# Six column tiles in the first pass, x over three queues, and a residual added on TensorE: one hybrid decoder step

## The chip, the core and the metric

The kernel runs on one core of a Trainium2 chip. The metric is the device time of one execution in microseconds (us). The engines are TensorE (PE, with PEld for its weight loads), VectorE (DVE), ScalarE (ACT), GpSimd (POOL) and SyncE (SP). SP, ACT and POOL can issue DMAs, each from a queue of its own.

## What is computed

One step of a one-layer decoder on 280 tokens: 16 meta tokens, 256 prompt tokens and 8 single tokens of running sequences. Everything is float32.

```python
u = rmsnorm(h, pre_mix_g)
proj = u @ w_in                      # 2048 -> 6672: z, x/B/C, dt, q, k, v, g
xbc = silu(causal_conv(xbc))         # width 4
# 16 Mamba-2 SSD heads beside 4 retention heads, chunked; states are returned
h = h + rmsnorm(mix @ w_out, post_mix_g)
f = rmsnorm(h, pre_ffn_g)
f = (silu(f @ w_gate) * (f @ w_up)) @ w_down     # 2048 -> 5632 -> 2048
h = h + rmsnorm(f, post_ffn_g)
```

## The kernel before

**Layout and products.** Features lie on the 128 partitions and tokens along the free dimension. Each float32 product is made of three fast matmuls (`three`, L129 to L133): weight and input are split into a rounded part (`hi`) and the rest (`lo`), and hi·hi, hi·lo and lo·hi are added up in PSUM. The weights are one stream of chunks of 8 blocks of 128x128 (`Stream.block`, L112). SP loads a chunk into `raw` (four buffers), ACT casts it to `hi` (L122), and DVE subtracts to get `lo` (L123); `hi` and `lo` have three buffers each. The first chunk is cut into four pieces.

**First pass.** `gemm("xb", ...)` (L336) makes 13 column tiles: `dt`, four tiles of B and C, eight of x. For its first columns it runs with `outer=4`: k is the outer loop, and for each of the 16 slabs of the input four columns are advanced at once in four PSUM banks, so that PE can start when the first slab is there. The other nine columns run one by one, 48 matmuls each. `prep(k)` (L163) loads two slabs of x on SP (L169), scales and splits each (ACT L170, DVE L171), squares them on ACT, and adds the squares up on POOL (L178). After the last slab two float32 matmuls (`pr`, L208) give the token norms, and `rbc` scales every eviction. `do_dt` (L247) is a generator: its long DVE chain on `dt`, transposes, a small DMA to memory and back (`lcd`, then four broadcasts `lcb`, L293 to L296), and `wj` (L304) are put in at columns 7, 8 and 9. `do_xbc` (L309) does the convolution of the other columns.

**Order of the work.** Each engine runs its instructions in one fixed order. A planner lays that order down ahead of time by priorities: program order, with some places moved ahead (`high_priority`, by 1500 for x and weights, 3000 for evictions). A wait on any engine holds back all that stands behind it there.

**Tail.** `gemm("d", ...)` (L883) makes 16 output columns; each eviction squares on ACT and scales on DVE into `o2` (L762, L763). `rstds` (L633, matmul L638) adds the squares up over the partitions and takes the root with Ln and Exp on ACT (L646, L648). Then the eight pairs of columns are multiplied by `rstd` (L895), the residual `hrs` is added (L903), and each pair is stored (L904, SP and ACT in turn). POOL does one of the eight multiplications and four of the eight additions, DVE the rest. The residual is loaded back from memory in eight loads (L888, issued by `load`, L85).

Of the kernel before, what the change touches and what calls it, by code (L numbers as in the profile page):

```python
# [15 lines left out]
P = 128  # L16
# [29 lines left out]
NEXTRA = 4  # L46
DECAY_ACT = False
WARM = 9
OUTF = 6


@with_exitstack
def hybrid_step(ctx: ExitStack, tc: tile.TileContext, wall, xT, pp, cc, dmask, cs, convst, ssm, ret,
# [16 lines left out]
    def slot(name, w=NA, n=4, dt=F32):  # L70
        return sp.tile([P, n, w], dt, name=name, tag="s")
# [12 lines left out]
    def load(out, in_):  # L84
        G.dma_start(out, in_)  # L85

    pps = cp.tile([P, NPP], F32, name="pps")
    nc.scalar.dma_start(pps, pp)
    ccs = cp.tile([P, NCC], F32, name="ccs")
    css = slot("css", NA, 2)  # L90

# [17 lines left out]
    class Stream:  # L109
        pos = 0  # L110

        def block(self):  # L112
            c, o = divmod(self.pos, CB)
            if o == 0:
                with tc.high_priority(offset=1500):
                    raw = st.tile([P, CB * P], F32, name=f"raw{c}", tag="raw", bufs=4)
                    self.hi = st.tile([P, CB * P], F32R, name=f"hi{c}", tag="hi")
                    self.lo = st.tile([P, CB * P], F32R, name=f"lo{c}", tag="lo")
                    w = CB * P // (4 if c == 0 else 1)
                    for f in range(0, CB * P, w):  # L120
                        nc.sync.dma_start(raw[:, f:f + w], wall[c, :, f:f + w])
                        A.copy(self.hi[:, f:f + w], raw[:, f:f + w])  # L122
                        V.tensor_tensor(self.lo[:, f:f + w], raw[:, f:f + w], self.hi[:, f:f + w].bitcast(F32), SUB)  # L123
            self.pos += 1
            return self.hi[:, o * P:(o + 1) * P], self.lo[:, o * P:(o + 1) * P]

# [33 lines left out]
    ul = [slot(f"ul{i}", dt=F32R) for i in range(4)]  # L160
    xsum = slot("xsum", NA, 2)

    def prep(k):  # L163
        i, j = divmod(k, 4)
        with tc.high_priority(offset=1500):
            for q in (j, j + 1):
                if k == 0 or q == j:
                    n = 1 if k == 0 else 2
                    nc.sync.dma_start(xs[i][:, q:q + n, :], xT[:, 4 * i + q:4 * i + q + n, :])  # L169
                A.activation(uh[i][:, q, :], xs[i][:, q, :], AF.Copy, scale=par("g_pre", 4 * i + q))  # L170
                V.scalar_tensor_tensor(ul[i][:, q, :], xs[i][:, q, :], par("g_pre", 4 * i + q),  # L171
                                       uh[i][:, q, :].bitcast(F32), MULT, SUB)
            if k == 0:
                A.activation(xsum, xs[i][:, j:j + 2, :], AF.Square)
            else:
                sq = slot(f"xq{k}", NA, 2)
                A.activation(sq, xs[i][:, j:j + 2, :], AF.Square)
                G.tensor_tensor(xsum, xsum, sq, ADD)  # L178

    ready = set()  # L180

# [23 lines left out]
    def token_norms():  # L205
# [12 lines left out]
    def pinned(out, in_):  # L218
        tc.keep_in_program_order(G.dma_start(out, in_))

    def const_loads():
        pace = cp.tile([P, 1], F32, name="pace0")
# [110 lines left out]
            do_xbc(m - 1, ps)  # L333

    held = {}
    gemm("xb", uin0, KT, NA, 0, 4, ev_first, outer=4, before=const_loads)  # L336
    for m in range(4, 13):
        gemm("xb", uin, KT, NA, m, m + 1, ev_first, pool=pm if m < 6 else pg)
        if 7 <= m < 10:
            next(held["dt"])  # L340
    load(oconv, cout.rearrange("p a b c -> p a (b c)"))
# [543 lines left out]
    hrs = []  # L885
    for k in range(0, KT, 2):
        hr = slot(f"hr{k}", NO, 2)
        load(hr, hd[:, k:k + 2, :])  # L888
        hrs.append(hr)
    pool_mul, pool_add = (7,), (0, 2, 4, 7)  # L890

    def scaled(n):
        ok = o2[n // 2][:, 2 * (n % 2):2 * (n % 2) + 2, :]
        e = G if n in pool_mul else V
        e.tensor_tensor(ok, ok, rstd.unsqueeze(1).to_broadcast([P, 2, NO]), MULT)  # L895

    scaled(7)
    for n in range(8):
        ok = o2[n // 2][:, 2 * (n % 2):2 * (n % 2) + 2, :]
        if n < 7:  # L900
            scaled(n)
        e = G if n in pool_add else V
        e.tensor_tensor(ok, ok, hrs[n], ADD)  # L903
        (nc.sync if n % 2 == 0 else nc.scalar).dma_start(yT[:, 2 * n:2 * n + 2, :], ok)  # L904


def _constants():
# [38 lines left out]
def _blocks(m, kouter=0):  # L946
    k, n = m.shape
    a = m.reshape(k // P, P, n // P, P).transpose(2, 0, 1, 3)
    if not kouter:
        return a.reshape(-1, P, P)  # L950
    return a.transpose(1, 0, 2, 3).reshape(-1, P, P)


def _layout(i):
    import numpy as np
    w = i["w_in"][0]
    z, xx, bb, cm = w[:, :1024], w[:, 1024:2048], w[:, 2048:2304], w[:, 2304:2560]
    dt, q, k, v, g = w[:, 2560:2576], w[:, 2576:3600], w[:, 3600:4624], w[:, 4624:5648], w[:, 5648:6672]
    first = np.concatenate([np.tile(dt, (1, 8)), bb, cm[:, :128]], 1)
    wo, wd = i["w_out"][0], i["w_down"][0]  # L960
    gu = np.stack([i["w_gate"][0].reshape(DM, FT, P), i["w_up"][0].reshape(DM, FT, P)], 2).reshape(DM, 2 * DFF)
    seq = [_blocks(first, 1), _blocks(np.concatenate([cm[:, 128:], xx], 1)), _blocks(k), _blocks(q), _blocks(v),
           _blocks(z), _blocks(g), _blocks(wo[:, :512], 1), _blocks(wo[:, 512:]), _blocks(gu[:, :P * OUTF], 1),
           _blocks(gu[:, P * OUTF:]), _blocks(wd)]
# [51 lines left out]
```

## Time and profile before

| | |
|---|---|
| median of three runs | 1280.14 us (1277.64 to 1282.41) |
| profiled execution | 1281.71 us, of which the span of the core 1279.9 us |
| PE, share of the span | 98% |
| DVE, ACT, POOL | 64%, 47%, 12% |
| chain that ended last | PE 95%, DMA 2%, DVE 1%, issue 1% |
| mean granted TensorE clock | 0.994 |

Busy shares are means over stages with different limits: where a stage waits is read from the waits and the timeline of that stage. Matmuls are pipelined, so that the rows show them overlapping; the pace is the distance between two starts.

### The profile page before, as it was taken

To read this page: it belongs to the slowest core of one execution; us is meant where nothing else is said; L and a number is where in the kernel's file an instruction comes from. 1 tells how busy PE (TensorE), PEld (TensorE's weight loads), DVE (VectorE), ACT (ScalarE), POOL (GpSimd) and SP (SyncE) were. 2 spreads that over 40 slices of the span, in tenths; PEclk is the share of its full clock that TensorE was granted. 3 is DMA by queue.
4 is the path that set the end of the run, shared out by engine and by line. 5 is a ranking of instruction groups with operands and counts; after the bars stand their busy time and mean duration, and the time that the engine had idled before them with its cause. 6 is when DMAs were issued, how large, how long until landed. Compare 5 with 4: busy or idle time off the path is not lost.

```text
span 1279.9 us, 24519 instructions
## 1 busy us (share of the span) xinstructions
PE 1254.4 (98%) x10078; PEld 1240.9 (97%) x10078; DVE 821.3 (64%) x1247; ACT 607.8 (47%) x826; POOL 153.1 (12%) x218
## 2 busy tenths in 40 slices
PE   8989999999999999999999999999999999999994
PEld 7989999999999999999999999999999999999994
DVE  7978779984775458566666666666666544444445
ACT  6665434445854446544444444444444433333331
POOL 3320001100001221101110110101101000000013
PEclk9999999999999999999999999999999999999997
DMA  8656347774466556577677766767676555555562
GB/s 271 206 190 215 121 147 260 273 260 144 136 214 230 182 180 217 183 244 245 229 236 247 246 231 231 248 215 248 214 247 229 183 181 181 182 182 181 181 223 93
DMA packets 74768, 266.41 MB, mean 208 GB/s; under 512 B 8528, under 2 KB 9440, under 8 KB 74656
## 3 DMA queue, kind: packets, MB, share of 16 engines
q1 hardware_dynamic: 60192, 214.17, 51.7%
q0 software_dynamic: 13744, 49.52, 10.7%
q8 instruction: 79, 1.29, 0.4%
q10 hardware_dynamic: 720, 1.16, 0.2%
q14 instruction: 33, 0.27, 0.1%
HBM read 246.15 MB, written 18.66 MB: 207 GB/s over the span
## 4 chain that ended last, share of the span: by engine, by line
PE 95%; DMA 2%; DVE 1%; issue 1%; SPq 0%; ACT 0%; POOL 0%; DVEq 0%; ACTq 0%
PE f L131 13%; PE f L133 13%; PE f L132 13%; PE d L132 7%; PE d L131 7%; PE d L133 7%; PE o L131 2%; PE o L132 2%; PE o L133 2%; PE xb L132 1%; PE xb L133 1%; PE xb L131 1%; PE k L131 1%; PE v L131 1%; PE v L132 1%; PE k L132 1%
## 5 line engine op out<-in xcount | busy, mean ns | idle before, releaser
L123 DVE TENSOR_TENSOR lo<-raw,hi 128x1024 fp32r<-128x1024 f32 (+1 forms) x405 | 492.3, 1217 | 357.8 <-ACT hi L122 353.1
L122 ACT CAST hi<-raw 128x1024 fp32r<-128x1024 f32 (+1 forms) x405 | 422.1, 1043 | 601.9 <-PE f L132 191.7
L131 PE MATMUL f<-fh,hi 128*128 128x264 f32 x1408 | 400.6, 285 | 0.0
L133 PE MATMUL f<-fh,lo 128*128 128x264 f32 x1408 | 399.3, 284 | 0.0
L132 PE MATMUL f<-fl,hi 128*128 128x264 f32 x1408 | 398.6, 283 | 0.0
L132 PEld LDWEIGHTS f<-fl,hi 128*128 128x128 f32 x1408 | 264.8, 188 | 0.3 <-issue 0.2
L131 PEld LDWEIGHTS f<-fh,hi 128*128 128x128 f32 x1408 | 264.8, 188 | 0.3 <-DVE f L863 0.2
L133 PEld LDWEIGHTS f<-fh,lo 128*128 128x128 f32 x1408 | 264.6, 188 | 0.0
L132 PE MATMUL d<-al,hi 128*128 128x264 f32 x704 | 200.2, 284 | 0.0
L131 PE MATMUL d<-ah,hi 128*128 128x264 f32 x704 | 199.7, 284 | 0.0
L133 PE MATMUL d<-ah,lo 128*128 128x264 f32 x704 | 199.4, 283 | 0.0
L131 PEld LDWEIGHTS d<-ah,hi 128*128 128x128 f32 x704 | 132.5, 188 | 0.0
L132 PEld LDWEIGHTS d<-al,hi 128*128 128x128 f32 x704 | 132.4, 188 | 0.0
L133 PEld LDWEIGHTS d<-ah,lo 128*128 128x128 f32 x704 | 132.3, 188 | 0.0
L131 PE MATMUL o<-mh,hi 128*128 128x264 f32 x256 | 72.8, 284 | 0.0
L132 PE MATMUL o<-ml,hi 128*128 128x264 f32 x256 | 72.6, 284 | 0.0
L133 PE MATMUL o<-mh,lo 128*128 128x264 f32 x256 | 72.4, 283 | 0.0
L869 POOL COPY pace<-f 128x1 f32<-128x1 f32 x25 | 28.6, 1144 | 362.2 <-DVE f L863 362.2
L858 DVE TENSOR_TENSOR f<-f,rhc 128x264 f32<-128x264 f32 x88 | 37.6, 432 | 49.1 <-PE f L133 48.8
L131 PE MATMUL xb<-uh,hi 128*128 128x280 f32 x208 | 61.8, 299 | 3.1 <-ACT hi L122 3.1
L133 PE MATMUL xb<-uh,lo 128*128 128x280 f32 x208 | 61.1, 297 | 3.4 <-DVE lo L123 3.4
L132 PE MATMUL xb<-ul,hi 128*128 128x280 f32 x208 | 61.7, 297 | 1.2 <-DVE ul L171 1.2
(296 smaller groups left out, 1983.2 us busy)
## 6 DMA issues: line engine op xcount, KB each, us to landing
raw<-in_dram SPq DMA_DIRECT2D x401, 512.0 KB, 3.6
rs<-in_dram POOLq DMA_DIRECT2D x16, 512.0 KB, 5.3
su<-in_dram POOLq DMA_DIRECT2D x16, 512.0 KB, 4.9
out_dram<-su POOLq DMA_DIRECT2D x16, 512.0 KB, 3.9
hb<-in_dram POOLq DMA_DIRECT2D x8, 512.0 KB, 5.9
hu<-in_dram POOLq DMA_DIRECT2D x8, 512.0 KB, 5.1
out_dram<-hu POOLq DMA_DIRECT2D x8, 512.0 KB, 4.1
lcb<-lcd POOLq DMA_DIRECT2D x4, 544.0 KB, 9.1
```

The costliest lines, as they stand in the source:

```text
L122: A.copy(self.hi[:, f:f + w], raw[:, f:f + w])
L123: V.tensor_tensor(self.lo[:, f:f + w], raw[:, f:f + w], self.hi[:, f:f + w].bitcast(F32), SUB)
L131: T.matmul(ps, hi, xhi, start=first, stop=False)
L132: T.matmul(ps, hi, xlo, start=False, stop=False)
L133: T.matmul(ps, lo, xhi, start=False, stop=last)
L858: V.tensor_tensor(t, ps, rhc, MULT)
L869: tc.keep_in_program_order(G.tensor_copy(pace, t[:, 0:1]))
```

## The change

In the first pass six columns are advanced at once (`OUTX = 6`; four PSUM banks of one pool and two of the other) and seven follow one by one; the weights are laid out to match. The first chunk is cut into three pieces. Slab 0 of x is loaded by SP, slabs 1 to 3 by ACT, the other twelve by POOL in pairs, each pair held back by a one-element copy on POOL that waits for the split of an earlier slab (`x_late`). The load of the parameters `pps` gets a high priority. The squares are added up by DVE instead of POOL.

In the tail the residual is loaded in four loads ahead of the last GEMM. For the first four pairs (eight columns) PE copies the residual into PSUM with an identity matmul and adds the scaled result with a second one, and ACT copies the sum back. DVE does all eight multiplications and the last four additions, POOL none. All stores go out from SP.

```diff
+OUTX = 6
+NPE = 4
@@ Stream.block
-                    w = CB * P // (4 if c == 0 else 1)
-                    for f in range(0, CB * P, w):
+                    cuts = (0, 2 * P, 4 * P, CB * P) if c == 0 else (0, CB * P)
+                    for f0, f1 in zip(cuts, cuts[1:]):
...
+    def x_loads():
+        nc.sync.dma_start(*xpart(0, 0, 1))
+        nc.scalar.dma_start(*xpart(0, 1, 2))
+        nc.scalar.dma_start(*xpart(0, 2, 4))
+    def x_late(k, parts):
+        pace = cp.tile([P, 1], F32, name=f"pacex{k}")
+        i, j = divmod(k, 4)
+        tc.keep_in_program_order(G.tensor_copy(pace, ul[i][:, j, 0:1].bitcast(F32)))
+        for p in parts:
+            pinned(*xpart(*p))
+    late = {0: ((1, 0, 2),), 1: ((1, 2, 4),), 2: ((2, 0, 2),), 4: ((2, 2, 4),), 6: ((3, 0, 2),), 8: ((3, 2, 4),)}
@@ prep
+            if k == 0:
+                x_loads()
...
-                    nc.sync.dma_start(xs[i][:, q:q + n, :], xT[:, 4 * i + q:4 * i + q + n, :])
...
+                if 4 * i + q in late:
+                    x_late(4 * i + q, late[4 * i + q])
...
-                G.tensor_tensor(xsum, xsum, sq, ADD)
+                V.tensor_tensor(xsum, xsum, sq, ADD)
@@ first pass
-    gemm("xb", uin0, KT, NA, 0, 4, ev_first, outer=4, before=const_loads)
-    for m in range(4, 13):
-        gemm("xb", uin, KT, NA, m, m + 1, ev_first, pool=pm if m < 6 else pg)
+    gemm("xb", uin0, KT, NA, 0, OUTX, ev_first, outer=OUTX, before=const_loads)
+    for m in range(OUTX, 13):
+        gemm("xb", uin, KT, NA, m, m + 1, ev_first, pool=pm if m == OUTX else pg)
@@ tail
+    hrs = []
+    for i in range(4):
+        hr = slot(f"hr{i}", NO)
+        load(hr, hd[:, 4 * i:4 * i + 4, :])
+        hrs.append(hr)
     ev, sums = ev_norm(o2, "g_pffn")
     gemm("d", ain, FT, NO, 0, KT, ev)
...
-    pool_mul, pool_add = (7,), (0, 2, 4, 7)
...
+    def residual(k):
+        sums_[k] = bank(f"h{k}", NO) if k % 2 else pg.tile([P, 512], F32, name=f"h{k}", tag="g")[:, :NO]
+        T.matmul(sums_[k], ident, hrs[k // 4][:, k % 4, :], start=True, stop=False)
+    for k in range(4):
+        residual(k)
+    for n in range(NPE):
+        scaled(n)
+        for k in (2 * n, 2 * n + 1):
+            ok = o2[k // 4][:, k % 4, :]
+            T.matmul(sums_[k], ident, ok, start=False, stop=True)
+            A.copy(ok, sums_.pop(k))
+        store(n)
+        for k in (2 * n + 4, 2 * n + 5):
+            if k < 2 * NPE:
+                residual(k)
+    for n in range(NPE, 8):
+        scaled(n)
+        ok = pair(o2, n)
+        V.tensor_tensor(ok, ok, pair(hrs, n), ADD)
+        store(n)
```

## Rows read from the trace of the kernel before

**Rows 1.** The waits of PE over the span: total us, times, longest us.
```profile
PE xb L133 <- DVE lo L123: 3.4, 1, 3.4
PE xb L131 <- ACT hi L122: 3.1, 2, 2.1
PE xb L132 <- DVE ul L171: 1.2, 2, 0.8
```
**Rows 2.** Timeline of PE, first pass: start, us, engine, line, operation; bracket: idle before.
```profile
4.55 0.38 PE L131 MATMUL xb<-uh,hi 128*128 128x280 f32 x1
...
11.42 0.40 PE L131 MATMUL xb<-uh,hi 128*128 128x280 f32 x1 [2.15 <-ACT hi L122]
...
13.30 0.29 PE L131 MATMUL xb<-uh,hi 128*128 128x280 f32 x1
...
17.94 0.29 PE L131 MATMUL xb<-uh,hi 128*128 128x280 f32 x1
...
35.30 1.10 PE L208 MATMUL pr<-xsum,ones 128*128 128x280 f32 x4
```
**Rows 3.** Timeline of ACT, first pass.
```profile
1.19 1.28 ACT L82 ACT_TABLE_LOAD   x1 [1.19 <-PEq L996]
3.52 0.53 ACT L170 ACTIVATE uh<-x,pps 128x280 fp32r<-128x280 f32 x1 [1.05 <-DMA pps<-in_dram]
...
10.33 1.04 ACT L122 CAST hi<-raw 128x1024 fp32r<-128x1024 f32 x1 [0.26 <-DMA raw<-in_dram]
```
**Rows 4.** Windows: stretch, its length, busy us by engine, PEclk, DMA share, GB/s.
```profile
3.00:9.00 6.00, 5.08 (x35) 4.71 (x34) 2.45 (x6) 3.27 (x9) 0.00 (x0) 1.00 0.83 231
9.00:10.00 1.00, 0.27 (x3) 0.04 (x1) 0.88 (x2) 1.00 (x3) 0.00 (x0) 1.00 1.03 417
```
**Rows 5.** Timeline of DVE and POOL, first pass.
```profile
9.12 0.93 DVE L171 SCALAR_TENSOR_TENSOR ul<-x,pps,uh 128x280 fp32r<-128x280 f32 x2 [1.36 <-ACT uh L170]
...
13.85 2.09 DVE L171 SCALAR_TENSOR_TENSOR ul<-x,pps,uh 128x280 fp32r<-128x280 f32 x2
...
14.22 1.40 POOL L178 TENSOR_TENSOR xsum<-xsum,xq 128x560 f32<-128x560 f32 x1 [2.71 <-ACT xq L177]
```
**Rows 6.** Waits between 78 and 97 us, then windows around that stall.
```profile
DVE wj L304 <- DMA lcb<-lcd: 6.2, 2, 3.9
...
89.10:92.50 3.40, 0.04 (x1) 0.00 (x0) 1.34 (x3) 3.37 (x6) 0.00 (x0) 1.00 0.11 43
92.50:96.40 3.90, 3.89 (x18) 3.90 (x19) 3.83 (x8) 3.49 (x6) 0.56 (x3) 0.56 0.74 190
```
**Rows 7.** A window of the columns made one by one, and its weight subtractions on DVE.
```profile
36.00:97.00 61.00, 57.64 (x429) 56.32 (x428) 52.30 (x116) 39.21 (x64) 14.34 (x40) 0.97 0.60 200
...
L123 DVE TENSOR_TENSOR lo<-raw,hi 128x1024 fp32r<-128x1024 f32 x17 | 20.7, 1223 | 3.4 <-ACT hi L122 3.3
```
**Rows 8.** Timeline of DVE and POOL in the tail.
```profile
1264.40 4.14 DVE L895 TENSOR_TENSOR p<-p,n5r 128x528 f32<-128x528 f32 x3 [1.24 <-ACT n5r L648]
...
1266.35 5.08 POOL L903 TENSOR_TENSOR p<-p,hr 128x528 f32<-128x528 f32 x3
...
1275.48 1.32 DVE L903 TENSOR_TENSOR p<-p,hr 128x528 f32<-128x528 f32 x2
```
**Rows 9.** The stores, from issue to landing.
```profile
DMA to landing us min/median/max: 2.0/2.1/2.2
```
**Rows 10.** PE after the last column of the output projection, and in the tail; ACT beside it.
```profile
476.67 1.03 PE L626 MATMUL ps<-vtok,ktok 128*128 128x256 f32 x4
477.69 0.71 PE L638 MATMUL n<-g_postq,ones 128*128 128x264 f32 x2
...
1262.24 0.39 ACT L762 ACTIVATE g_pffnq<-d 128x264 f32<-128x264 f32 x1 [7.87 <-PE d L133]
1262.69 0.71 PE L638 MATMUL n<-g_pffnq,ones 128*128 128x264 f32 x2
```
**Rows 11.** The loads of the residual: us of issue, first and last start.
```profile
L85 POOL DMA_DIRECT2D hr<-hd x8: 539/540/578, 1215.4 to 1249.2; - x8
```
**Rows 12.** A window of the tail.
```profile
1267.00:1270.00 3.00, 0.00 (x0) 0.00 (x0) 3.00 (x2) 0.00 (x0) 3.00 (x3) 0.51 0.24 90
```

More of the change, by code (lines that the diff above doesn't have):

```diff
@@ L85, in load, with pinned @@
         G.dma_start(out, in_)
+    def pinned(out, in_):
+        tc.keep_in_program_order(G.dma_start(out, in_))
     pps = cp.tile([P, NPP], F32, name="pps")
-    nc.scalar.dma_start(pps, pp)
+    with tc.high_priority(offset=6000):
+        nc.scalar.dma_start(pps, pp)
     ccs = cp.tile([P, NCC], F32, name="ccs")
@@ L118, in block @@
                     self.lo = st.tile([P, CB * P], F32R, name=f"lo{c}", tag="lo")
-                    w = CB * P // (4 if c == 0 else 1)
-                    for f in range(0, CB * P, w):
-                        nc.sync.dma_start(raw[:, f:f + w], wall[c, :, f:f + w])
-                        A.copy(self.hi[:, f:f + w], raw[:, f:f + w])
-                        V.tensor_tensor(self.lo[:, f:f + w], raw[:, f:f + w], self.hi[:, f:f + w].bitcast(F32), SUB)
+                    cuts = (0, 2 * P, 4 * P, CB * P) if c == 0 else (0, CB * P)
+                    for f0, f1 in zip(cuts, cuts[1:]):
+                        nc.sync.dma_start(raw[:, f0:f1], wall[c, :, f0:f1])
+                        A.copy(self.hi[:, f0:f1], raw[:, f0:f1])
+                        V.tensor_tensor(self.lo[:, f0:f1], raw[:, f0:f1], self.hi[:, f0:f1].bitcast(F32), SUB)
             self.pos += 1
@@ L161, in hybrid_step, with xpart @@
     xsum = slot("xsum", NA, 2)
+    def xpart(i, q0, q1):
+        return xs[i][:, q0:q1, :], xT[:, 4 * i + q0:4 * i + q1, :]
+    def x_loads():
[9 more added lines that the diff above has]
+    late = {0: ((1, 0, 2),), 1: ((1, 2, 4),), 2: ((2, 0, 2),), 4: ((2, 2, 4),), 6: ((3, 0, 2),), 8: ((3, 2, 4),)}
     def prep(k):
@@ L165, in prep @@
         with tc.high_priority(offset=1500):
+            if k == 0:
+                x_loads()
             for q in (j, j + 1):
-                if k == 0 or q == j:
-                    n = 1 if k == 0 else 2
-                    nc.sync.dma_start(xs[i][:, q:q + n, :], xT[:, 4 * i + q:4 * i + q + n, :])
                 A.activation(uh[i][:, q, :], xs[i][:, q, :], AF.Copy, scale=par("g_pre", 4 * i + q))
@@ L216, in token_norms @@
             A.mul(tabs[:, 2 + i, :], tabs[:, i, :], 1.0 / 16.0)
-    def pinned(out, in_):
-        tc.keep_in_program_order(G.dma_start(out, in_))
     def const_loads():
@@ L884, in hybrid_step, with pair, store @@
     (rstd,) = rstds("n5", [[sums["a"], sums["b"]]], 1.0 / DM, load_table=False)
[L885 to L889, printed above, removed]
-    pool_mul, pool_add = (7,), (0, 2, 4, 7)
-    def scaled(n):
[L893 to L904, printed above, removed]
+    def pair(tiles, n):
+        return tiles[n // 2][:, 2 * (n % 2):2 * (n % 2) + 2, :]
+    def scaled(n):
+        ok = pair(o2, n)
+        V.tensor_tensor(ok, ok, rstd.unsqueeze(1).to_broadcast([P, 2, NO]), MULT)
+    def store(n):
+        nc.sync.dma_start(yT[:, 2 * n:2 * n + 2, :], pair(o2, n))
+    sums_ = {}
+    def residual(k):
[15 more added lines that the diff above has]
+        scaled(n)
+        ok = pair(o2, n)
+        V.tensor_tensor(ok, ok, pair(hrs, n), ADD)
+        store(n)
 def _constants():
@@ L958, in _layout @@
     dt, q, k, v, g = w[:, 2560:2576], w[:, 2576:3600], w[:, 3600:4624], w[:, 4624:5648], w[:, 5648:6672]
-    first = np.concatenate([np.tile(dt, (1, 8)), bb, cm[:, :128]], 1)
+    xbc = np.concatenate([np.tile(dt, (1, 8)), bb, cm, xx], 1)
     wo, wd = i["w_out"][0], i["w_down"][0]
     gu = np.stack([i["w_gate"][0].reshape(DM, FT, P), i["w_up"][0].reshape(DM, FT, P)], 2).reshape(DM, 2 * DFF)
-    seq = [_blocks(first, 1), _blocks(np.concatenate([cm[:, 128:], xx], 1)), _blocks(k), _blocks(q), _blocks(v),
+    seq = [_blocks(xbc[:, :P * OUTX], 1), _blocks(xbc[:, P * OUTX:]), _blocks(k), _blocks(q), _blocks(v),
            _blocks(z), _blocks(g), _blocks(wo[:, :512], 1), _blocks(wo[:, 512:]), _blocks(gu[:, :P * OUTF], 1),
```

## The prediction, made before the changed kernel was seen

> **What bounds the kernel now.** I first read the engines' shares: PE is busy for 98% of the span, so a change can give back only what PE loses. The waits of PE [rows 1] list all of that between its first matmul and its last but for fragments: one wait of 3.4 us on a `lo` and four that add up to 4.3 us, all in the first pass. Then I read the timeline at the two ends. At the start [rows 2]: the first product begins at 4.55 us and the four-column phase ends at 35.30 us, where `pr` starts. From 13.30 to 17.94 us PE runs undisturbed: 12 blocks of three matmuls in 4.64 us, 0.129 us a matmul. The phase has 4 x 16 x 3 = 192 of them, 24.8 us; it took 30.75, so 6.0 us are lost (the waits above and small delays that are no wait on the list). At the other end [rows 8]: from 1264.40 us on, PE has nothing to do, and DVE works alone on the path until 1276.8 us; the last store lands some 2 us later [rows 9]. Between these ends the GEMMs hide everything else.
>
> **The first pass: what the start loses.** Of the 6.0 us, chunk 1 of the weights costs most. The first 24 matmuls need only chunk 0; the 25th starts at 11.42 us, since the chunk's cast began at 10.33 us, just when its load had landed [rows 2, 3]. Ideal would be 4.55 + 24 x 0.129 = 7.65 us, so 3.8 us are lost up to there and 6.0 - 3.8 = 2.2 us after it. With six columns a slab takes 18 matmuls, but chunk 0 still holds just 24 matmuls' work, so the start still hangs on when chunk 1 lands. Ahead of it the same bytes are needed as before. What can move is how densely they are carried: from 3 to 9 us the DMA engines were busy at 0.83 and moved 231 GB/s [rows 4], so 6 x 0.17 = 1.0 us of their time was unused. With SP freed of slabs 1 to 3 it issues chunk 1 some three issues sooner. I take 0.8 us; the bounds are 1.0 us and, if POOL's first late pair (slabs 4 and 5, asked for once slab 0 is split) now runs ahead of chunk 1, a loss of 280 KB at 231 GB/s, 1.2 us.
>
> This is a place where a rule speaks against the change. The Trainium skill ("DMA: Bandwidth & Descriptors", section "Rules for kernel authors") says that spreading loads over SP, ACT and GpSimd gives no bandwidth, as all run on the same 16 engines, and saves issue time alone. By that rule the 0.8 us would be nothing and the sum 0.8 us smaller, a rival below; the second row of the windows, 417 GB/s from the same single queue in the tenth microsecond, sides with the rule, the 0.83 of the first speaks for some issue time to be saved.
>
> **The first pass: after chunk 1.** Of the 2.2 us, 1.2 are waits on `ul` [rows 1], and the small delays beside them I put down to the same queue of DVE. Two `ul` take 0.93 us together while POOL is idle and 2.09 us while POOL adds squares [rows 5]. The change ends that: POOL's seven additions go to DVE. DVE's own price for one is bounded by its 128x528 additions in the tail, spaced 0.62 us when POOL was done and 1.8 when it was not [rows 8]; I take 0.7. Per slab DVE then does 0.75 of a chunk (1.22 us each [rows 7], so 0.92), one `ul` (0.47) and half an addition (0.35): 1.74 us of PE's 18 x 0.129 = 2.32. DMA needs 384 + 140 KB per slab, 231 GB/s against the 417 it can do. So both keep up, and I count 1.9 of the 2.2 us as saved. Six columns themselves remove no matmul: 624 stay 624.
>
> The rest of this part I cost at nothing, with its cover. ACT issues two loads of x ahead of its 1.28 us table load: 1.19 + 0.84 + 1.28 = 3.3 us, covered by the wait for `pps` until 3.52 us [rows 3]; 0.2 us are to spare. The six one-element copies on POOL stand ahead of the later pairs of x and of `const_loads`; each waits for a slab at least four ahead of the pair it releases, and a slab lasts PE 2.32 us, so a pair has over 8 us. First pass: 0.8 + 1.9 = 2.7 us saved, from -0.3 (late pair in the way, half of the rest) to 1.0 + 2.2 = 3.2.
>
> **The middle: a stall that the change moves.** At 89.1 us PE loses 3.4 us and then runs until 96.4 us at a mean granted clock of 0.56, half speed for most of it: 18 matmuls in 3.9 us instead of 2.3, 1.6 us more [rows 6]. Its `lo` stood on DVE behind `wj`, which waited 6.2 us for the `lcb` broadcasts. With six columns `dt` is evicted two columns, 12 us of PE work, later, less what the start gains; the chain through `dt`, `lcd` and `lcb` moves with it, toward the first k columns. The planner places `wj` anew, by its own idea of when `lcb` lands. Nothing shortens the chain, so I take the stall as unchanged: 0, bounded by -5.0 us (it vanishes) and by the second rival.
>
> **The tail.** DVE's 528-wide operation costs 1.8 us beside POOL and 0.62 to 0.70 alone [rows 8]. After the change POOL is still, and DVE has 8 multiplications and 4 additions: 12 x 0.62 + 0.08 = 7.5 us, from 1264.40 to 1271.9 instead of 1276.8: 4.9 us. The other branch: the first pair is ready at 1265.1; PE then has 8 sums and 4 residuals to do in float32. Two such matmuls (four records) took about 1.0 us in the middle, one alone 0.71 with its latency [rows 10]; at 0.45 each, 12 take 5.4 us, to 1270.5, and ACT's last copy 0.39 after that [rows 10]: 1271.1 with the gaps between. DVE ends last, but by 0.8 us only.
>
> Two things eat into the 4.9 us. The planner can slip residual matmuls in front of the last norm matmul, which waits for ACT's square: after the output projection it did so with two `ps` matmuls, and the norm matmul started a microsecond after they did [rows 10] instead of the 0.45 us that ACT's square alone takes here; I take 0.45 us. And stores: before they went out over 9 us and each landed 2.1 us after issue [rows 9]; now four or five of 264 KB follow within 2 us on SP alone, in order, so that one that waits for ACT holds those behind it. At the 300 to 400 GB/s of the start that is 0.7 to 0.9 us each; I take 0.6 us of queueing. Tail: 4.9 - 0.45 - 0.6 = 3.85 us saved; from 4.9 to 0.3 (fourth rival). The residual's loads move from 1215 us and later [rows 11] to before the last GEMM, on a POOL queue that is idle there: nothing, covered by 250 us of PE work.
>
> **Sum.** 2.7 + 0 + 3.85 = 6.55 us. The profiled execution took 1281.71 us, so 1275.2 for it; it lies 1.57 us above the median of 1280.14, so I forecast 1273.6 us. A measurement of this kernel tells 0.5%, 6.4 us, from no change: the line is at 1273.7, and the forecast stands on it. Its own range is 1272.0 (first pass and tail both at their good ends, 3.2 and 4.9) to 1276.6 (first pass at its bad end).
>
> **Rivals.** First, the stall in the middle goes away, because `wj` lands behind enough finished `lo`: 5.0 us more, 1268.6. For it: it hung on one ordering. Against: the chain is as long as before.
>
> Second, the other side: DVE falls behind in the columns made one by one. From 36 to 97 us it did 52.3 us of work, 20.7 of them 17 `lo` [rows 7]. Now seven columns remain, 14 `lo` (17.1 us) and the same 31.6 of other work: 48.7 us against 7 x 48 x 0.129 + 2.5 (the float32 matmuls between) = 45.9 of PE. It was ahead before and is now 2.8 us behind, and the 6.2 us wait comes on top: if PE must wait for both, 9.0 in place of 3.4, and half clock for as long again, it costs 5.6 + 1.6, and 1280.8 us is slightly slower than before. It decides as soon as the planner lets convolution work ahead of `lo`. Against it: `lo` has priority, and the convolutions can slide into the k columns.
>
> Third, the queues bring nothing and the start stays bound to chunk 1 at 11.4 us: 0.8 us less, 1274.4; with POOL's pair in its way and half of the DVE gain lost as well, 1276.6.
>
> Fourth, PE's clock falls in the tail. Before, with PE idle from 1263.4 us, the granted clock was 0.51 between 1267 and 1270 [rows 12], its 1.2 GHz level. The 12 float32 matmuls would take 0.9 us each, 10.8 in all, and end at 1276.5 with ACT's copy: the tail saves 0.3, and the time is 1277.2. Against it: the matmuls themselves keep PE busy from 1265 us on.
>
> **Chances.** Forecast 0.45, split about evenly at the line; first rival 0.15; second 0.15, a third of it slower by over 0.5% should waits add up beyond the price; third 0.15; fourth 0.10. Faster by over 0.5%: 0.22 + 0.15 + a third of the third rival, 0.05: 0.42. Slower by over 0.5%: 0.05. Within: 0.53. The range reaches from the first rival to the fourth and most of the second: 1268 to 1280.
>
> **What would show it.** `pr` at 35.30 + 12.4 - 2.7 = 45.0 us, with the 25th matmul near 10.6 us; `ul` at 0.47 us each throughout; no PE wait on `ul`. In the tail 12 DVE operations of 0.62 us and the last addition 7.5 to 8 us after `rstd`; stores that land within 3 us of it. I would be wrong if chunk 1 landed later than 10.3 us, if PE's total wait between 45 and 110 us differed much from 3.4 us, or if the last store came from ACT's copies instead of DVE.

## The result, and the profile after

| | before | after |
|---|---|---|
| median of the runs beside each other | 1279.37 us (1277.64 to 1282.41, 4 runs) | 1271.57 us (1271.00 to 1272.85, 4 runs) |
| profiled execution | 1281.71 us, span 1279.9 | 1271.0 us, span 1269.2 |
| mean granted TensorE clock | 0.994 | 1.0 |

The ratio is 0.9938, with an interval of 0.9917 to 0.9959: the changed kernel is 0.6% faster. The forecast was 1273.6 us, with 1268 to 1280 around it; the time came out 2.0 us below it. It also lies 0.4 us below the forecast's own range of 1272.0 to 1276.6; only the wider range, with the rivals in it, holds it.

First the engines' shares of after:

```profile
PE 1261.2 (99%) x10110; PEld 1247.3 (98%) x10110; DVE 812.7 (64%) x1254; ACT 605.2 (48%) x829; POOL 138.3 (11%) x214
```

PE is still the bound. What it loses has become less, and the list of its waits shows where (total us, times, longest us):

```profile
PE xb L137 <- ACT hi L128: 1.7, 2, 0.9
PE warm L113 <- DVE ones L111: 1.1, 1, 1.1
PE n L660 <- DVE rqs L714: 0.2, 1, 0.2
```

Beside [rows 1], both the wait on `lo` (3.4 us) and the waits on `ul` (1.2 us) are gone, and the one on the first casts fell from 3.1 to 1.7 us. That wait is another one now: both parts of it (0.93 and 0.74 us) are for the second and third piece of chunk 0, while ACT took up chunk 1, at 9.48 us, without waiting for its load. (The `warm` wait lies before the first product, in both kernels.)

To see how much each stage gave, I follow PE's timeline at the seams. After:

```profile
4.92 0.84 PE L137 MATMUL xb<-uh,hi 128*128 128x280 f32 x2
...
45.08 1.10 PE L233 MATMUL pr<-xsum,ones 128*128 128x280 f32 x4
...
92.32 0.29 PE L137 MATMUL k<-uh,hi 128*128 128x280 f32 x1
...
468.45 0.61 PE L660 MATMUL n<-g_posts,ones 128*128 128x264 f32 x2
...
479.78 0.47 PE L137 MATMUL f<-fh,hi 128*128 128x264 f32 x1
...
1000.00 0.28 PE L137 MATMUL d<-ah,hi 128*128 128x264 f32 x1
...
1255.79 0.60 PE L660 MATMUL n<-g_pffns,ones 128*128 128x264 f32 x2
```

The six-column phase (the slab phase: slab by slab, all its columns at once) ends at 45.08 us. Before, the four-column phase ended at 35.30 us [rows 2]; two more columns are 96 matmuls of 0.129 us, so the same point is 47.7 us. The table reads the other seams of the two profiled executions in the same way; its column "gained in the stage" is what the stage itself gave.

| seam | before | after | gained in the stage | forecast |
|---|---|---|---|---|
| end of the slab phase, `pr` (six columns) | 47.7 us | 45.08 us | 2.6 | 2.7 |
| first `k` matmul | 100.08 | 92.32 | 5.2 | 0 |
| norm after the output projection | 476.23 | 468.45 | 0.0 | 0 |
| first `d` matmul, after the `f` GEMM | 1005.67 | 1000.00 | -2.1 | 0 |
| last norm, after the `d` GEMM | 1261.99 | 1255.79 | 0.5 | 0 |
| end of the span | 1279.93 | 1269.23 | 4.5 | 3.85 |

The first row is no fixed size. The old start ended its slab phase at 35.30, 34.94 and 34.69 us in three profiles (before, and two runs below that share its first pass), the new one at 44.87 to 46.10 us in five; on the scale of the table that is a gain of anything from 1.0 to 2.8 us.

The rows add up to 10.7 us, but the medians differ by 7.8 only. The two profiled executions are not typical in the same way: that of before, 1281.71 us, lies 1.6 us above the 1280.14 it was read against (2.3 above 1279.37), that of after 0.6 below its median: 10.7 - 2.3 - 0.6 = 7.8.

**The middle.** The windows of after (length, busy us by engine, PEclk, DMA share, GB/s) show no stall between 78 and 98 us:

```profile
78.00:98.00 20.00, 20.00 (x156) 19.61 (x156) 15.90 (x36) 12.49 (x25) 7.18 (x20) 1.00 0.67 218
```

PE is busy for all 20 us at full clock, where before it stood for 3.4 us and then ran at 0.56 for 3.9 us [rows 6]. `wj` still waits for its broadcasts on DVE, though. DVE's timeline of after, the `lo` and `wj` of that stretch:

```profile
90.65 1.22 DVE L129 TENSOR_TENSOR lo<-raw,hi 128x1024 fp32r<-128x1024 f32 x1
94.53 0.17 DVE L326 TENSOR_TENSOR wj<-lcb,lct 128x12 f32<-128x12 f32 x1 [2.67 <-DMA lcb<-lcd]
96.14 0.17 DVE L326 TENSOR_TENSOR wj<-lcb,lct 128x12 f32<-128x12 f32 x1
96.68 1.22 DVE L129 TENSOR_TENSOR lo<-raw,hi 128x1024 fp32r<-128x1024 f32 x1
98.10 0.17 DVE L326 TENSOR_TENSOR wj<-lcb,lct 128x12 f32<-128x12 f32 x1 [0.20 <-DMA lcb<-lcd]
```

From one `lo` to the next, 90.65 to 96.68, 6.0 us pass. In the profile of before it was 10.6 us, from DVE's timeline, with the matmul of PE that waited:

```profile
80.59 1.23 DVE L123 TENSOR_TENSOR lo<-raw,hi 128x1024 fp32r<-128x1024 f32 x1 [0.58 <-ACT hi L122]
...
91.23 1.22 DVE L123 TENSOR_TENSOR lo<-raw,hi 128x1024 fp32r<-128x1024 f32 x1
...
92.51 0.40 PE L133 MATMUL xb<-uh,lo 128*128 128x280 f32 x1 [3.36 <-DVE lo L123]
```

How long can PE go on without a new `lo`? By count, a chunk is 24 matmuls, 24 x 0.129 = 3.1 us of PE, and three `lo` buffers make 9.3 us. The trace gives less. PE stood from 92.51 - 3.36 = 89.15 us, 8.56 us after the last `lo` had begun, and the next one takes 1.28 us from its start until PE goes on. So in this profile two `lo` could have started 8.56 - 1.28 = 7.28 us apart without a wait, and 10.64 - 7.28 is the 3.36 us of the wait. The 6.0 us of after lie below that.

**The tail.** DVE's timeline of after:

```profile
1258.29 3.80 DVE L919 TENSOR_TENSOR p<-p,n5r 128x528 f32<-128x528 f32 x6 [1.33 <-ACT n5r L670]
1262.01 1.32 DVE L946 TENSOR_TENSOR p<-p,hr 128x528 f32<-128x528 f32 x2
1263.25 1.32 DVE L919 TENSOR_TENSOR p<-p,n5r 128x528 f32<-128x528 f32 x2
1264.49 1.31 DVE L946 TENSOR_TENSOR p<-p,hr 128x528 f32<-128x528 f32 x2
```

ACT's timeline there, its last copies:

```profile
1262.92 1.71 ACT L938 COPY p<-h 128x264 f32<-128x264 f32 x4 [0.96 <-PE h L937]
```

DVE ends at 1265.80 us, 7.5 us after it began, against 12.4 before [rows 8]: 4.9 us less. ACT is done 1.2 us earlier. PE's timeline there, right behind the first norm matmul at 1255.79 us:

```profile
1256.23 0.61 PE L929 MATMUL h<-hr,ccs 128*128 128x264 f32 x2
1256.68 0.61 PE L660 MATMUL n<-g_pffnq,ones 128*128 128x264 f32 x2
```

And the stores, from issue to landing:

```profile
DMA to landing us min/median/max: 2.0/2.2/2.5
```

One residual matmul does stand between the two norm matmuls, as feared, but the time from the first of them to DVE's start grew only from 2.41 us (1261.99 to 1264.40) to 2.50. From DVE's end to the end of the span it is 3.4 us instead of 3.1. So 4.9 - 0.1 - 0.3 = 4.5 us. The clock did not fall; the windows of after across the tail (PEclk is the third number from the end):

```profile
1258.00:1262.00 4.00, 4.00 (x18) 3.13 (x17) 3.71 (x6) 1.77 (x5) 0.00 (x0) 1.00 0.13 48
1262.00:1266.00 4.00, 2.22 (x10) 1.54 (x9) 3.80 (x7) 1.51 (x4) 0.00 (x0) 1.00 0.85 323
```

### The profile page after: what moved, and what is told of

Its sections match the earlier page's. It is cut to its first block, busy times and chain, and to the rows that moved or that the text cites. A ratio compares the mean times of both kernels' runs of the same rounds, so it can differ in the third digit from the quotient of the medians.

```text
span 1269.2 us, 24570 instructions
## 1 busy us (share of the span) xinstructions
PE 1261.2 (99%) x10110; PEld 1247.3 (98%) x10110; DVE 812.7 (64%) x1254; ACT 605.2 (48%) x829; POOL 138.3 (11%) x214
## 4 chain that ended last, share of the span: by engine, by line
PE 98%; DVE 1%; DMA 0%; ACT 0%; issue 0%; SPq 0%; DVEq 0%
PE f L137 14%; PE f L138 14%; PE f L139 13%; PE d L137 7%; PE d L138 7%; PE d L139 7%; PE o L137 2%; PE o L138 2%; PE o L139 2%; PE xb L139 2%; PE xb L138 2%; PE xb L137 2%; PE k L137 1%; PE v L137 1%; PE k L139 1%; PE v L139 1%
```

## The experiments

My theory after this reading was: the gain is made of a better start, of the stall that is no longer there because `wj` stands at another place among the `lo`, and of a tail that DVE ends in 7.5 us. The rivals were that six columns themselves, the three queues or the squares on DVE make the gain, and that the tail slows the `f` GEMM.

### The two halves alone

The first is the changed kernel with the tail of before; the second is the kernel before with the part of the change's diff that stands under its tail, and nothing else.

```diff
@@ first: tail as before
-    hrs = []
-    for i in range(4):
-        hr = slot(f"hr{i}", NO)
-        load(hr, hd[:, 4 * i:4 * i + 4, :])
-        hrs.append(hr)
...
+    pool_mul, pool_add = (7,), (0, 2, 4, 7)
...
+        e = G if n in pool_add else V
+        e.tensor_tensor(ok, ok, hrs[n], ADD)
+        (nc.sync if n % 2 == 0 else nc.scalar).dma_start(yT[:, 2 * n:2 * n + 2, :], ok)
@@ second: first pass as before, with
+    for k in range(4):
+        residual(k)
+    for n in range(NPE):
+        scaled(n)
...
+    for n in range(NPE, 8):
+        scaled(n)
+        ok = pair(o2, n)
+        V.tensor_tensor(ok, ok, pair(hrs, n), ADD)
+        store(n)
```

> Only the first-pass half of the change; the tail is the old one. In the trace of the changed kernel the k stage starts 7.8 us earlier than before: 2.7 us from the start (pk at 58.4 against 61.1 us) and 5.1 us because the stall behind wj is gone. Theory (both belong to the first pass and recur in every run): k starts at 92 to 93 us, no wait of PE on lo over 0.5 us before 110 us, time 7 to 8 us under before, about 1272 us. Rival (the stall was a chance of one profiled run of before): k starts early here too, but the median gains only some 2.7 us, about 1276.5. If the f GEMM, 518.0 us before and 520.1 after, is slowed by the first pass, it takes 520 us here and the gain is 2 us smaller.

> Only the tail half of the change; the first pass is the old one. Theory: the start is that of before (pr at 35.3 us), the stall of PE on lo behind wj near 89 us is there again with 3 to 3.5 us of waiting and half clock after it, k starts near 100 us; from the last norm matmuls of the tail to the end 13.4 us instead of 17.9, so about 4.5 us less, 1275 us. If the f GEMM is slowed by the tail's earlier residual loads and their buffers, it takes 520 us here instead of 518 and the gain is 2.4 us, about 1277. Rival (stall by chance): no wait on lo near 89 us in this trace, though the first pass is the old one.

The first half alone took 1276.24 us (1275.64 to 1276.99), ratio 0.9967 [0.9954, 0.9980]; the tail alone 1276.90 us (1272.24 to 1278.34), 0.9975 [0.9956, 0.9994]; before beside them 1280.51 us. So 4.3 and 3.6 us, together 7.9: the halves add up to the whole, within intervals of some 2 us on either side. Both times missed what I expected. The first half gained 4.3 us and not 7 to 8, which by the time alone is nearest to my rival (1276.5 us, a stall by chance); its trace, with the early `k`, speaks for the theory. The tail alone came out 1.9 us above the 1275 us that I expected with `f` unchanged. Whether the stall was chance is read from the trace of the tail alone and from the next run. The waits of PE in the run with the new tail alone:

```profile
PE xb L134 <- DVE lo L124: 3.1, 1, 3.1
PE xb L132 <- ACT hi L123: 1.6, 1, 1.6
PE xb L133 <- DVE ul L172: 1.2, 2, 0.8
```

The old first pass brings the stall with it, 3.1 us and half clock behind it; the first half alone has none (its first `k` matmul starts at 92.09 us, as in the changed kernel). `f` took 518.0 us with the new tail alone and 520.1 with the new first pass alone, so the tail is not what slows it.

### The stall, taken away without six columns, and put back

The kernel before, with the three steps of `do_dt` put in at columns 9 to 11 instead of 7 to 9, and nothing else:

```diff
-        if 7 <= m < 10:
+        if 9 <= m < 12:
             next(held["dt"])
```

> The kernel before with one edit: the three later steps of the dt generator are put in at columns 9, 10 and 11 instead of 7, 8 and 9. Four columns at once, old tail. Theory (the stall hangs on where wj and the lcb loads come in relation to lo, not on the six columns as such): the wait of PE on lo shrinks from 3.4 us to under 1, no half clock near 93 us, k starts near 95 us, time 4 to 5 us under before, about 1275 us. Rival (the stall follows the chain wherever it is put): the wait of 3 us or more reappears later by two columns, about 12 us, and the time is that of before, about 1279.5 us.

It took 1275.49 us (1275.32 to 1275.99), ratio 0.9962 [0.9947, 0.9977]: 5.0 us less than before, for one line. All the waits of PE in it are at the start:

```profile
PE xb L131 <- ACT hi L122: 3.3, 2, 2.5
PE warm L107 <- DVE ones L105: 1.1, 1, 1.1
```

The longest time from `lo` to `lo` was 5.3 us (88.49 to 93.74). POOL issues the first of the four broadcast loads at 84.19 us here and the last `lo` ahead of `wj` starts 4.3 us later; in the profile of before it started 1.4 us later (79.16 and 80.59), so that nearly the whole wait fell between two `lo`. Against the profile of before this run is 6.1 us ahead at the first `k` matmul (93.97 against 100.08), 0.6 of it from the start, and stays so to the end (6.3). The reverse is the changed kernel with four columns:

```diff
-OUTX = 6
+OUTX = 4
...
-        gemm("xb", uin, KT, NA, m, m + 1, ev_first, pool=pm if m == OUTX else pg)
+        gemm("xb", uin, KT, NA, m, m + 1, ev_first, pool=pm if m < 6 else pg)
```

> The changed kernel with OUTX = 4: four columns at once, but x on three queues, squares on DVE and the new tail. Theory (the six columns moved the dt chain against the weights, which ended the stall; the queues and DVE's squares alone shorten the start): the start saves 2 to 3 us of the 6.0 (pr at 32.5 to 33.5 us instead of 35.3), and the stall of PE on lo behind wj is there again with 2 us or more plus half clock; time 3 to 5 us above the changed kernel, 1275 to 1276.5 us. Rival (the stall is ended by POOL's silence or the queues): no wait over 1 us, and the time within 1.5 us of 1271.6.

Here the stall is back. DVE's timeline of this run:

```profile
78.02 1.23 DVE L129 TENSOR_TENSOR lo<-raw,hi 128x1024 fp32r<-128x1024 f32 x1 [0.58 <-ACT hi L128]
83.56 0.17 DVE L326 TENSOR_TENSOR wj<-lcb,lct 128x12 f32<-128x12 f32 x1 [4.31 <-DMA lcb<-lcd]
85.28 0.16 DVE L326 TENSOR_TENSOR wj<-lcb,lct 128x12 f32<-128x12 f32 x1
87.47 0.17 DVE L326 TENSOR_TENSOR wj<-lcb,lct 128x12 f32<-128x12 f32 x1 [0.82 <-DMA lcb<-lcd]
87.56 1.22 DVE L129 TENSOR_TENSOR lo<-raw,hi 128x1024 fp32r<-128x1024 f32 x1
```

And its windows, the wait of PE and the time behind it:

```profile
86.50:88.83 2.33, 0.08 (x1) 0.00 (x0) 1.46 (x4) 2.32 (x5) 0.00 (x0) 1.00 0.33 127
88.83:93.00 4.17, 4.17 (x20) 4.17 (x21) 3.70 (x8) 4.12 (x7) 0.56 (x3) 0.59 0.67 178
```

Three `wj` stand in a row between two `lo`, 9.5 us apart (78.02 to 87.56); in the changed kernel only two do. The count alone does not decide, though: with `dt` later three stand there too, but DVE waits less for them (2.5 us in all against 5.6 here). PE stands for 2.3 us and then runs at a granted clock of 0.59. Its slab phase ended at 32.68 us against 35.30 before, the same 2.6 us that six columns showed. The median, 1271.97 us (1270.59 to 1274.29), is lower than the 1275 to 1276.5 that I expected, and only 0.2 to 0.4 us above the changed kernel: by the time of its runs this experiment does not bear the theory out, only by its trace. The profiled run was the slowest of the five, and `f` took 518.5 us in it, 1.6 less than in the changed kernel.

The third step keeps four columns, moves the `dt` steps as above, and loads x on SP as in the next experiment:

```diff
-OUTX = 6
+OUTX = 4
...
-        if 7 <= m < 10:
+        if 9 <= m < 12:
```

> Four columns at once, x on SP alone, squares on DVE, the new tail, and the three later steps of the dt generator at columns 9 to 11. Theory (six columns are worth only the stall that they moved; with the stall moved otherwise, four do as well): pr at 32 to 33 us, no wait of PE over 1 us between 30 and 110 us, k starts within 1 us of the 91.6 us that it had with six columns and x on SP, and the time lies within 1 us of the six-column version, about 1269 to 1270 us. Rival (six columns also save time by themselves, through the lower rate of loads per us of PE): k starts at 93 us or later and the time is 1.5 us or more above.

It took 1269.45 us (1269.15 to 1269.92), 0.9921 [0.9907, 0.9934], against 1268.85 us for the same kernel with six columns on the same chip. PE waits for nothing between 30 and 110 us, and `k` starts at 92.38 us. So six columns were worth the moved stall, and 0.6 us beside it. The slab phase ended at 33.09 us, 2.2 us sooner than before; with x on SP the six columns gained 3.4 and 4.9 us in two profiles, so there they do bring a better start as well.

So the stall follows the place of `wj`, not the number of columns: 10.6, 10.4 and 9.5 us from `lo` to `lo` in the three profiles that have it (before, the tail alone, four columns), 5.3 to 7.0 in the eleven that don't (6.0 after, 5.3 with `dt` later, 7.0 with four columns and `dt` later). In all three PE ran dry 8.56 us after the last `lo` had begun, and the time from `lo` to `lo` less 7.3 us gives the wait of each: 3.4, 3.1 and 2.3 us. The three builds with the stall also scatter most: over 7.5 us before (1276.24 to 1283.78 beside the first of these runs), 6.1 with the tail alone and 3.7 with four columns, against 0.7 and 0.8 for the two with `dt` later. The 12 runs of before fall into five from 1276.24 to 1277.70 us and seven from 1280.51 to 1283.78, and of the eight with the tail alone those of 1272.24 and 1274.22 us have a mean granted clock of 0.999, the other six (1276.68 to 1278.34) 0.995 to 0.998. That the stall is short or missing in some executions would explain all this; only one execution of each was profiled, so this is argued and not shown.

### x on SP's queue alone

The changed kernel with x loaded as before, all from SP in the order of need, without the paced loads on POOL and those on ACT:

```diff
-            if k == 0:
-                x_loads()
             for q in (j, j + 1):
+                if k == 0 or q == j:
+                    n = 1 if k == 0 else 2
+                    nc.sync.dma_start(*xpart(i, q, q + n))
...
-                if 4 * i + q in late:
-                    x_late(4 * i + q, late[4 * i + q])
```

> The changed kernel with x loaded as before by SP alone, between the weights; six columns, squares on DVE, new tail. Theory (the queues bring chunk 1 forward): chunk 1 of the weights lands near 10.3 us instead of 9.5, the 25th matmul starts 0.8 to 1.5 us later than in the changed kernel, pr at 45.8 to 46.5 instead of 45.1, time about 1 us above, 1272.5 us. Rival (all queues share the same engines, so nothing is gained): chunk 1 lands at 9.5 us as in the changed kernel and the time is the same within 0.3 us.

It took 1269.09 us (1268.30 to 1269.74), 0.9916 [0.9896, 0.9936]. As this beat both kernels, it went to another chip beside the changed kernel:

> The changed kernel once more, as the measure for the other three of this call. Expected 1271.6 us; the trace with pr near 45.1 us and f at 520.1 us, since both came out within 0.2 us in every build that shares its first pass. Rival (f's pace changes from run to run): f anywhere between 517.9 and 520.1.

> The changed kernel with x on SP alone once more, beside the changed kernel on the same chip. Theory (x on three queues costs time: it holds up the end of chunk 0 at the start, and the build has a slower f): 2 to 3 us below the changed kernel, about 1269 us, f at 517.9 us, pr near 44.3. Rival (the first measurement was a good day): within 1 us of the changed kernel.

There x on SP took 1268.85 us (1268.06 to 1268.99), 0.9914 [0.9901, 0.9928], and the changed kernel 1271.80 us (1270.64 to 1272.94), 0.9937 [0.9925, 0.9950]. So the three queues don't gain; the version without them is 2.9 us faster. The measure itself missed one expectation: its `pr` came at 45.90 us and not near 45.1 (`f` took 520.1 us, as expected). ACT's timeline shows what the start has to do with it. After:

```profile
1.18 0.45 ACTq L175 DMA_DIRECT2D x<-in_dram  x1
1.66 0.45 ACTq L176 DMA_DIRECT2D x<-in_dram  x1
...
6.24 0.40 ACT L128 CAST hi<-raw 128x256 fp32r<-128x256 f32 x1 [1.36 <-DMA raw<-in_dram]
...
8.32 0.62 ACT L128 CAST hi<-raw 128x512 fp32r<-128x512 f32 x1 [1.24 <-DMA raw<-in_dram]
...
9.48 1.05 ACT L128 CAST hi<-raw 128x1024 fp32r<-128x1024 f32 x1
```

With x on SP, the run on the second chip:

```profile
5.97 0.91 ACT L128 CAST hi<-raw 128x256 fp32r<-128x256 f32 x2
7.43 1.05 ACT L128 CAST hi<-raw 128x1024 fp32r<-128x1024 f32 x1 [0.55 <-DMA raw<-in_dram]
```

ACT's second load, slabs 2 and 3, is issued at 1.66 us and travels beside chunk 0, whose last piece then is cast from 8.32 us; with x on SP the last two pieces are cast from 5.97 us on. In the other profiles of the two kernels the last piece alone is cast from 7.70 us, and the last two with x on SP from 6.17. The cast of chunk 1 starts at 9.48 us against 7.43, but at 9.00 against 9.10 in the other two profiles: it varies. The only wait of PE left in this run is the one before its first product, and the slab phase ends at 42.83 us instead of 45.08 (44.31 in the other profile). 1.8 us of that still stand after the output projection (466.68 against 468.45 us). `f` then adds 2.2 (517.9 us instead of 520.1, for which see below), and 0.7 are lost again by the end of the span, 1265.9 against 1269.2 us. The two other profiles, held against each other at the same seam, give 0.8 (468.43 against 469.25), and 468.43 against 468.45 gives nothing. So `f`, whose cause is open, is the steady part of the 2.9 us; the start gives between 0 and 2.6. Whether ACT's load or POOL's first pair is what delays chunk 0 was not separated.

A finer cut of chunk 1 on top of it, in two pieces:

```diff
-                    cuts = (0, 2 * P, 4 * P, CB * P) if c == 0 else (0, CB * P)
+                    cuts = (0, 2 * P, 4 * P, CB * P) if c == 0 else (0, 4 * P, CB * P) if c == 1 else (0, CB * P)
```

> The version with x on SP alone, and chunk 1 of the weights cut into two pieces with a load, cast and subtraction each. Theory (the start is bound by the landing of chunk 1, 9.1 us there): the first piece lands 0.7 to 1.2 us sooner, the 25th matmul starts near 9.2 instead of 10.2 us, pr at 43.3 to 43.8 instead of 44.3, time 0.5 to 1 us below the version with x on SP, about 1268.3 us. Rival (PE is then held by ACT's and DVE's fixed cost of the pieces or by the slabs of x): pr at 44.3 or later and no gain.

1268.90 us (1268.71 to 1269.60), 0.9917 [0.9903, 0.9930]: no gain over 1268.85. The two pieces were cast from 7.61 us on, where the whole chunk was cast from 7.43 us in one profile and from 9.10 in the other; its landing varies more between executions than a cut can give. `pr` came at 43.46 us, between the 42.83 and 44.31 of the two profiles without the cut.

### The squares back on POOL

```diff
-                V.tensor_tensor(xsum, xsum, sq, ADD)
+                G.tensor_tensor(xsum, xsum, sq, ADD)
```

> The changed kernel with the squares of x added up by POOL as before. Theory (with six columns DVE has room): ul takes about 1.0 us where POOL adds and 0.47 elsewhere, DVE needs 1.9 to 2.0 us of the 2.32 of a slab, PE waits for no ul over 0.3 us, pr within 0.5 us of 45.1 and the time within 1 us of 1271.6. Rival (the squares are what ended the waits on ul): waits of PE on ul of 0.5 us and more come back as before, pr at 46 us or later and 1 to 2 us more.

1271.41 us (1270.79 to 1272.25), 0.9934 [0.9910, 0.9958]; with the squares on DVE it was 1271.57 and 1271.80. DVE's timeline in this run:

```profile
14.26 1.65 DVE L194 SCALAR_TENSOR_TENSOR ul<-x,pps,uh 128x280 fp32r<-128x280 f32 x1
```

And POOL's:

```profile
13.82 1.78 POOL L203 TENSOR_TENSOR xsum<-xsum,xq 128x560 f32<-128x560 f32 x1
```

A `ul` beside POOL's addition again took 1.65 us instead of 0.50, yet no matmul of PE waited for one. With six columns a slab feeds PE for 2.3 us instead of 1.55, and that can cover it. `pr` came at 45.90 us, 0.8 later than I expected, as in the second profile of the changed kernel, which has the squares on DVE.

### All additions on DVE

The changed kernel with no residual on PE, so that DVE does eight multiplications and eight additions:

```diff
-NPE = 4
+NPE = 0
...
-    for k in range(4):
-        residual(k)
```

> The changed kernel with NPE = 0: in the tail DVE does all eight multiplications and all eight additions, PE and ACT nothing, POOL nothing. Theory (the tail is bound by the count of DVE operations at 0.62 us each, and most of the gain comes from POOL's silence): 16 operations instead of 12, DVE ends 2.5 us later after rstd (10.0 instead of 7.5 us), time 2.0 to 2.5 us above the changed kernel, about 1274 us. Rival (the gain comes from TensorE's part of the additions): DVE's operations take longer than 0.62 us each or the time is 4 us or more above the changed kernel.

1274.48 us (1273.38 to 1274.83), 0.9951 [0.9935, 0.9968]: 2.7 to 2.9 us more than the two medians of the changed kernel, 1271.80 and 1271.57. DVE's timeline, the first and the last of its operations in the tail:

```profile
1259.82 1.33 DVE L919 TENSOR_TENSOR p<-p,n5r 128x528 f32<-128x528 f32 x2 [1.24 <-ACT n5r L670]
...
1268.48 1.32 DVE L944 TENSOR_TENSOR p<-p,hr 128x528 f32<-128x528 f32 x2
```

And a window of the tail:

```profile
1262.00:1266.00 4.00, 0.00 (x0) 0.00 (x0) 4.00 (x7) 0.00 (x0) 0.00 (x0) 0.50 0.58 222
```

Sixteen operations take 10.0 us, twelve took 7.5: the 2.5 us are the four additions that PE and ACT carry. (The rest of the 2.7 to 2.9 lies within the spread of the runs, and the start of this profile was a slow one, with `pr` at 46.10 us.) So of DVE's 12.4 us before, 2.4 went with POOL's work beside it, although DVE took over all that POOL had done, and 2.5 with the half that PE took. With PE idle the granted clock is 0.50 here, and nothing is lost by it, as no matmul is left.

### The pace of the `f` GEMM

The `f` GEMM took 518.0 us before and 520.1 after, without a wait in either. A window of the `f` tiles alone, in the kernel before:

```profile
600.00:700.00 100.00, 100.00 (x828) 100.00 (x828) 14.66 (x34) 7.37 (x18) 7.39 (x6) 1.00 0.71 241
```

The same window of after:

```profile
600.00:700.00 100.00, 100.00 (x825) 100.00 (x824) 15.07 (x35) 7.08 (x17) 6.21 (x5) 1.00 0.71 234
```

And with x on SP, the run on the second chip:

```profile
600.00:700.00 100.00, 100.00 (x828) 100.00 (x827) 15.27 (x36) 7.05 (x17) 6.20 (x5) 1.00 0.69 233
```

PE is busy throughout at full clock, but after starts 825 matmuls in 100 us where the other two start 828; over the 4224 of `f` that is 1.9 us, nearly all of the 2.1. One theory was the place of the buffers: the six one-element tiles of the paced loads shift all that is allotted after them, by their sizes an odd multiple of 64 bytes. Two unused tiles more make it a multiple of 128:

```diff
+    for i in range(2):
+        G.memset(cp.tile([P, 1], F32, name=f"pad{i}"), 0.0)
```

> The changed kernel with two unused one-column tiles more, which move all buffers allocated behind them by 64 bytes, so that the blocks of weights and inputs start again at multiples of 128 bytes, as in the kernel before; the six tiles of x_late had moved them by 192. No other instruction is changed. Theory (the f GEMM's 520.1 us against 518.0 come from where its operands lie): f takes about 518 us again and the time is 1 to 2 us below the changed kernel, about 1270 us. Rival (it is not the offset within 128 bytes but which of the large buffers hold which tile, or something else of the first pass): f takes 520 us and the time is 1271.6.

1272.42 us (1270.85 to 1272.83), 0.9940 [0.9920, 0.9961], and `f` took 520.0 us: the theory falls. (No trace shows the addresses; the shift is counted from the sizes of the tiles.) The lengths of `f` in all profiles fall into three groups: 517.9 to 518.0 (before, tail alone, `dt` later, x on SP, chunk 1 cut), 518.5 (both with `OUTX = 4`), and 519.6 to 520.1 (all with six columns and paced loads). Two profiles of the same kernel agree to 0.1 us (520.1 twice; 517.9 twice, on two chips). So it belongs to the build (the kernel as compiled), not to the run; which part of the build makes it stays open.

## Why the forecast came near, and where it was wrong

**The total came near by luck, because errors partly cancel.** 6.55 us were forecast; the medians show 7.8 and the two profiles 10.7. The stall that I left in place is worth 5.0 us (the run with `dt` later); the `f` GEMM, which I took as untouched, gave 2.1 back; and the profiled execution of before lay 2.3 us above the median beside the changed kernel, where I had reckoned 1.57.

**The first pass: the size was near, the path wrong.** 2.6 us in the profile for 2.7 forecast, but 1.8 in the second profile of the same kernel (`pr` at 45.90 us); all five of this first pass give 1.0 to 2.8. Chunk 1 was cast from 9.48 us, 0.85 earlier than before, as forecast, and the 25th matmul started at 10.97 us for 10.6 forecast. Yet the start no longer hung on when chunk 1 lands, as I had it: ACT did not wait for that load at all, and PE's two waits were for the second and third piece of chunk 0. And the cause I gave, SP freed by the other queues, is not borne out: with x on SP alone chunk 1 was cast from 7.43 and 9.10 us, with three queues from 9.48 and 9.00. The other term, 1.9 us from DVE freed of POOL, is covered twice: with six columns the squares may stay on POOL at no cost, and with four columns and the squares on DVE the slab phase gained the same 2.6 us. I had added up one edit's gain and taken the other as neutral ("six columns themselves remove no matmul"), where with x on three queues either one alone would do. `ul` came at 0.46 to 0.51 us each, and no matmul waited for one, as said.

**The third rival was right about the queues, and too mild.** The Trainium skill ("DMA: Bandwidth & Descriptors", section "Rules for kernel authors") says that loads spread over several issuing engines share the same 16 DMA engines. The runs agree: x on one queue lost nothing. They point further: with slabs of x on other queues beside it, chunk 0's last piece was cast from 8.32 and 7.70 us, against the last two from 5.97 and 6.17 without, and the first `k` matmul came at 92.32 and 93.14 us against 90.07 and 91.57. That the loads needed later hold up chunk 0 fits this; which of them does it was not tested.

**The middle: the step that failed.** "Nothing shortens the chain, so I take the stall as unchanged." My sign of being wrong came true: between 45 and 110 us PE waited for nothing, in place of 3.4 us. The chain indeed got no shorter in kind: the broadcasts still landed 5.7 to 9.7 us after issue (6.6 to 11.7 before), and `wj` still waited 3.4 us in all (6.2 before). But the stall was never the chain's length; it was the time from one `lo` to the next on DVE against what the buffers cover. That sum was there to be made from the trace of before: 10.6 us against 7.3. A new order of `wj` and `lo` undoes it, as the changed kernel (6.0) and the two runs with `dt` later (5.3 and 7.0) show. The first rival named just this ("`wj` lands behind enough finished `lo`") with a chance of 0.15, and put the price at 5.0 us; the run that moved `dt` by two columns measured 5.0 between medians. The chance was far too low. The second rival, DVE behind in the single columns, did not show: after 10 us PE waited for no `lo` at all.

**The tail: right in its main term, too careful in the others.** DVE's twelve operations took 7.5 us as forecast. The planner's slip cost 0.1 us and not 0.45, since only one residual matmul stood between the norm matmuls and it ran while ACT's square was under way; queueing of the stores cost 0.3 and not 0.6. So 4.5 instead of 3.85. By medians the tail alone gave 3.6. The last store came from DVE, as forecast, 1.2 us behind ACT's last copy, and the clock stayed at 1.00, so the fourth rival did not happen.

**What the prediction had no term for** is the 2.1 us in `f`. Nothing in the trace of before shows it, since it belongs to the changed build alone. Nor had it one for the clock at the start, which differs between executions of one kernel (below).

The fastest version that the runs found is the changed kernel with x on SP, 1268.85 us, 2.9 us below the changed kernel.

## What to carry to other kernels

Where a wait for a DMA stands on an engine that also prepares the weights, add up the time from one preparation to the next and hold it against what the buffers cover, read from the trace of a stall where there is one (7.3 us here, where the count of buffers says 9.3); moving the waiting step by a little is the cheapest experiment there is (one line, 5.0 us here). For loads that are needed in a known order, try one queue in that order before spreading them: here it lost nothing and was 2.5 and 2.9 us faster, though only part of that is the start. When two edits relieve the same loss, count it once, and test each with the other undone.

## What the hardware showed that I had not expected

A GEMM of 4224 matmuls that PE runs without a wait at full clock took 517.9 to 520.1 us in different builds of the same loop, and the same to 0.1 us in the two executions each of two builds.

After a wait of PE near the start the granted clock fell to the lower level (1.2 GHz) in some executions and not in others, of one and the same kernel too. A window of the changed kernel's first profile, where PE had waited 0.93 us before 6.69 and waited 0.74 before 8.99, and the same window of its second, where it had waited 1.89 us before 7.39:

```profile
7.40:10.90 3.50, 2.68 (x19) 2.23 (x18) 1.24 (x3) 2.58 (x5) 0.66 (x2) 1.00 1.03 421
...
7.40:10.90 3.50, 3.50 (x15) 3.50 (x16) 2.42 (x4) 3.39 (x7) 1.19 (x2) 0.51 1.01 412
```

At the lower level PE started 15 matmuls where the other execution started 19, though that one still waited in between, and the slab phase ended at 45.90 us instead of 45.08. The run with the squares on POOL (a wait of 2.09 us, a clock of 0.51, `pr` at 45.90 us) did the same. The length of the wait alone does not tell it: in the profile of before PE waited 2.15 us before 11.42 [rows 2] and the clock stayed at 1.00, and with `dt` later it waited 2.49 us before 11.63 and the clock was 0.50 from 12 to 14 us.
